# An embedding lookup with position add: the scheduled loop against five hand-written instruction streams

## The chip, the cores and the metric

The kernel runs on one core of a Trainium2 chip. The metric is the device time of one execution in microseconds (us). A profile covers one execution; its *span* runs from the first to the last instruction that it records. Differences of 2% count as faster or slower, smaller ones as the same.

Runs were made on several chips. The jobs fall into two kinds, told apart by SyncE's records at the end of the kernel: in one kind (called *slow SyncE* below, which is not the slow state of a run) they stand 0.70 us apart, in the other they take 7 to 28 ns. Times are therefore compared only within one job, where the kernel before was run beside the others; where two jobs are set side by side, the text says so.

## The reference

```python
batch, seq_len, vocab_size, d_model = 32, 512, 50000, 512
def reference(indices, embedding_table, position_embed):
    token_embed = embedding_table[indices]            # 32 x 512 rows of 512 floats
    return (token_embed + position_embed).astype(np.float32)
```

Rows of 2 KB are gathered (33.5 MB), the position rows added, and the result stored (33.5 MB).

## The kernel before

It is written for a scheduler (a tile framework) that puts in all waits. GpSimd gathers 128 rows for each instruction, VectorE adds, SyncE stores. A data tile holds up to four gathers; 20 tiles rotate. The waits are on *semaphores*, counters that one engine or DMA raises and another waits for.

```python
const = ctx.enter_context(tc.tile_pool(name="const", bufs=1))
data_pool = ctx.enter_context(tc.tile_pool(name="data", bufs=BUFS))   # BUFS = 20
# ... cut: load indices, transpose them, copy the position rows to PSUM (pos_ps)
def chunk(b, parts):
    at = 0
    for n in parts:
        data = data_pool.tile([P, n, D], f32, tag="data")
        for j in range(n):
            k = at + j
            where = idx0[:, 2 * k : 2 * k + 1] if b == 0 else idx_t[:, k, b : b + 1]
            nc.gpsimd.indirect_dma_start(out=data[:, j, :], out_offset=None, in_=table,
                in_offset=bass.IndirectOffsetOnAxis(ap=where, axis=0))
            nc.vector.tensor_tensor(out=data[:, j, :], in0=data[:, j, :],
                                    in1=pos_ps[k][:], op=add)
        nc.sync.dma_start(out=out_rows[b][:, at : at + n, :], in_=data[:])
        at += n
# batches 0, 1, 31: parts (1,1,1,1); 2 to 5 and 30: (2,2); all others: (4,)
```

## Time and profile before

| | |
|---|---|
| time, median of 3 runs | 184.62 us (184.57 to 184.68) |
| span of the profiled execution | 176.2 us |
| time of that same execution | 177.94 us |

The last two rows belong to one execution, the first to others.

These lines are from the profile page of the kernel before: the span, three rows of the span in 40 slices (busy tenths, and GB/s), the DMA packets, the chain of waits by engine, and the two costliest groups of instructions.

```profile
span 176.2 us, 480 instructions
...
POOL 3777777777777777777777777777777756777300
DMA  4889999999999999999999999999999999999995
GB/s 131 305 236 354 384 380 387 414 410 406 417 378 397 413 413 407 402 404 390 419 419 415 415 421 412 415 413 414 419 420 416 415 408 421 406 399 406 413 411 205
DMA packets 17635, 68.33 MB, mean 388 GB/s; under 512 B 3008, under 2 KB 3008, under 8 KB 14560
...
DMA 57%; POOL 27%; issue 11%; DVE 2%; POOLq 0%; DVEq 0%
...
L88 POOL DMA_INDIRECT data<-in_embedding_table_dram,idx_t x124 | 117.2, 945 | 39.8 <-issue 33.7
L94 DVE TENSOR_TENSOR data<-data,pos_ps 128x512 f32<-128x512 f32 x128 | 86.9, 687 | 79.6 <-DMA data<-in_embedding_table_dram,idx_t 72.7
```

DMA is at 9 tenths from the third slice to the next-to-last one. GpSimd (POOL) is at 7 tenths, and its idle time is mostly "issue": it waits for nothing that the profile shows.

This is the table of stages of the kernel before. The last two numbers of a line are the mean busy share of the DMA engines and GB/s.

```profile
0.00:5.00 5.00, 0.56 (x4) 0.55 (x4) 0.52 (x1) 1.73 (x2) 2.28 (x8) 1.00 0.48 141
10.00:15.00 5.00, 0.00 (x0) 0.00 (x0) 2.14 (x4) 0.00 (x0) 3.78 (x5) 1.00 0.93 275
40.00:60.00 20.00, 0.00 (x0) 0.00 (x0) 11.17 (x17) 0.00 (x0) 15.13 (x17) 1.00 1.02 402
140.00:160.00 20.00, 0.00 (x0) 0.00 (x0) 10.84 (x16) 0.00 (x0) 13.70 (x15) 1.00 1.02 410
170.00:174.00 4.00, 0.00 (x0) 0.00 (x0) 1.20 (x2) 0.00 (x0) 0.00 (x0) 1.00 1.01 397
174.00:175.00 1.00, 0.00 (x0) 0.00 (x0) 0.00 (x0) 0.00 (x0) 0.00 (x0) 1.00 0.19 72
175.00:176.20 1.20, 0.00 (x0) 0.00 (x0) 0.00 (x0) 0.00 (x0) 0.00 (x0) 1.00 0.00 0
```

The transfers run at full rate until 174 us and are over before 175 us. What follows is the *end*: 1.2 us without any transfer, in which the engines close down together.

The timeline of GpSimd in the kernel before, near its only stall (start, duration, instruction, idle time before it):

```profile
143.31 0.94 POOL L88 DMA_INDIRECT data<-in_embedding_table_dram,idx_t  x1 [0.35 <-issue]
146.37 0.95 POOL L88 DMA_INDIRECT data<-in_embedding_table_dram,idx_t  x1 [2.12 <-issue]
147.63 0.95 POOL L88 DMA_INDIRECT data<-in_embedding_table_dram,idx_t  x1 [0.30 <-DMA out_dram<-data]
```

And two lines of the kernel's closing instructions (source line 132, where the framework closes): duration in ns, minimum, median and maximum, then first and last start.

```profile
L132 SPq EVENT_SEMAPHORE  x12: 17/28/28, 172.3 to 176.2; - x12
L132 POOLq DRAIN  x3: 40/102/10675, 161.4 to 176.0; - x3
```

SyncE (SPq) goes through its twelve closing waits at 17 to 28 ns each.

### The profile page before, as it was taken

What the parts mean: (1) busy time and instruction counts of PE and PEld (TensorE: products, weight loads), DVE (VectorE), ACT (ScalarE), POOL (GpSimd) and SP (SyncE); (2) the same over time, 40 slices, a digit from 0 to 9 for tenths busy, and PEclk for the clock granted to TensorE, in tenths of its full rate; (3) what the DMA queues carried; (4) which work ended last, traced back from release to release, by engine and by line L of the source; (5) the groups of instructions that cost most, each with busy time, mean ns of one, the idle gap of its engine ahead of it and who ended that gap; (6) DMA issues with size and microseconds to landing.
All of it is one profiled execution on the core that took longest, in us unless ns stands there. A gap on an engine that the chain in (4) does not pass through costs nothing.

```text
span 176.2 us, 480 instructions
## 1 busy us (share of the span) xinstructions
PE 0.7 (0%) x4; PEld 0.6 (0%) x4; DVE 87.7 (50%) x130; ACT 3.6 (2%) x5; POOL 121.7 (69%) x134
## 2 busy tenths in 40 slices
PE   0100000000000000000000000000000000000000
PEld 0100000000000000000000000000000000000000
DVE  1162554454744447354466464544647464444740
ACT  2410000000000000000000000000000000000000
POOL 3777777777777777777777777777777756777300
DMA  4889999999999999999999999999999999999995
GB/s 131 305 236 354 384 380 387 414 410 406 417 378 397 413 413 407 402 404 390 419 419 415 415 421 412 415 413 414 419 420 416 415 408 421 406 399 406 413 411 205
DMA packets 17635, 68.33 MB, mean 388 GB/s; under 512 B 3008, under 2 KB 3008, under 8 KB 14560
## 3 DMA queue, kind: packets, MB, share of 16 engines
q0 software_dynamic: 10240, 33.56, 50.2%
q1 hardware_dynamic: 7392, 34.74, 48.1%
q14 instruction: 3, 0.02, 0.0%
HBM read 34.74 MB, written 33.55 MB: 388 GB/s over the span
## 4 chain that ended last, share of the span: by engine, by line
DMA 57%; POOL 27%; issue 11%; DVE 2%; POOLq 0%; DVEq 0%
DMA data<-in_embedding_table_dram,idx_t 56%; POOL data L88 27%; DVE data L94 2%; DMA idx<-in_indices_dram 1%; POOLq L88 0%; DVEq L94 0%
## 5 line engine op out<-in xcount | busy, mean ns | idle before, releaser
L88 POOL DMA_INDIRECT data<-in_embedding_table_dram,idx_t x124 | 117.2, 945 | 39.8 <-issue 33.7
L94 DVE TENSOR_TENSOR data<-data,pos_ps 128x512 f32<-128x512 f32 x128 | 86.9, 687 | 79.6 <-DMA data<-in_embedding_table_dram,idx_t 72.7
L88 POOL DMA_INDIRECT data<-in_embedding_table_dram,idx x4 | 4.0, 993 | 2.7 <-DMA idx<-in_indices_dram 1.7
L79 ACT COPY pos_ps<-pos_sb 128x512 f32<-128x512 f32 x4 | 2.4, 589 | 4.9 <-DMA pos_sb<-in_position_embed_dram 4.8
L68 DVE CAST idx_f<-idx_raw 32x512 f32<-32x512 int32 x1 | 0.5, 523 | 3.8 <-DMA idx_raw<-in_indices_dram 3.8
L79 ACT ACT_TABLE_LOAD x1 | 1.3, 1283 | 0.8 <-PEq L121 0.8
L75 DVE CAST idx_t<-turned 128x128 int32<-128x128 f32 x1 | 0.3, 292 | 0.8 <-PE turned L73 0.8
L73 PE MATMUL turned<-ident,idx_f 32*128 32x32 f32 x4 | 0.7, 300 | 4.4 <-DVE idx_f L68 4.4
L73 PEld LDWEIGHTS turned<-ident,idx_f 32*128 32x128 f32 x4 | 0.6, 206 | 4.4 <-issue 4.4
L121 POOL MEMSET const-float32-0.0<- 128x1 f32 x1 | 0.1, 105 | 0.3 <-issue 0.3
L60 POOL MEMSET ones<- 32x32 f32 x1 | 0.1, 114 | 0.3 <-POOLq L121 0.3
L62 POOL TENSOR_SCALAR_AFFINE_SELECT ident<-ones 32x32 f32<-32x32 f32 x1 | 0.2, 202 | 0.1
L121 POOL MEMSET const-uint8-127<- 128x1 uint8 x1 | 0.1, 122 | 0.0
L121 POOL MEMSET const-bfloat16-1.0<- 128x1 bf16 x1 | 0.1, 116 | 0.0
L121 POOL MEMSET const-float32-1.0<- 128x1 f32 x1 | 0.1, 108 | 0.0
## 6 DMA issues: line engine op xcount, KB each, us to landing
out_dram<-data SPq DMA_DIRECT2D x24, 1024.0 KB, 7.7
out_dram<-data SPq DMA_DIRECT2D x10, 512.0 KB, 6.9
out_dram<-data SPq DMA_DIRECT2D x12, 256.0 KB, 5.8
data<-in_embedding_table_dram,idx_t POOLq DMA_INDIRECT x124, 7.7
pos_sb<-in_position_embed_dram SPq DMA_DIRECT2D x4, 256.0 KB, 4.7
idx_raw<-in_indices_dram SPq DMA_DIRECT2D x1, 128.0 KB, 2.5
data<-in_embedding_table_dram,idx POOLq DMA_INDIRECT x4, 4.7
idx<-in_indices_dram SPq DMA_DIRECT2D x1, 4.0 KB, 1.8
```

Of the source, the lines that this page charges most:

```text
L60: nc.gpsimd.memset(ones[:], 1.0)
L62: nc.gpsimd.affine_select(out=ident[:], in_=ones[:], pattern=[[-1, B]], compare_op=mybir.AluOpType.is_equal, fill=0.0, base=0, channel_mul ...
L68: nc.vector.tensor_copy(out=idx_f[:].rearrange("b p k -> b (p k)"), in_=idx_raw[:, :, 0])
L73: nc.tensor.transpose(turned[:, k, :], idx_f[:, :, k], ident[:])
L75: nc.vector.tensor_copy(out=idx_t[:], in_=turned[:])
L79: nc.scalar.copy(out=pos_ps[k][:], in_=pos_sb[k][:])
L88: nc.gpsimd.indirect_dma_start(out=data[:, j, :], out_offset=None, in_=table, in_offset=bass.IndirectOffsetOnAxis(ap=where, axis=0),)
L94: nc.vector.tensor_tensor(out=data[:, j, :], in0=data[:, j, :], in1=pos_ps[k][:], op=add)
L121: nc = _bacc.Bacc("TRN2", target_bir_lowering=False, num_devices=1)
```

## The change

The intent is to take waiting and scheduling into the author's hands: one critical section, five instruction streams, a semaphore for each purpose, at most one wait on an instruction. There are 24 full slots instead of 20 tiles and 16 completion lanes for gathers instead of the framework's 8 (a *slot* is a buffer for one batch of four gathers; a *lane* is a semaphore that says that a gather has landed, and gathers take the lanes in turn). Stores are issued from ScalarE. Gathers, adds, store sizes and bytes stay.

```diff
-BUFS = 20
+SLOTS = 24
+LANES = 16
 ...
+    with tc.tile_critical():
+        nc.sync.dma_start(out=idx0[:], in_=idx_first).then_inc(s_first, 16)
 ...
+        for g in range(B * K):                                   # GpSimd
+            b, k = divmod(g, K)
+            if b >= SLOTS and k == 0:
+                nc.gpsimd.wait_ge(s_out[b - SLOTS], 16 * done)
+            ins = nc.gpsimd.indirect_dma_start(out=slots[b % SLOTS][:, k, :], ...
+            ).then_inc(s_gather[g % LANES], 16)
+            if g >= LANES:
+                ins._wait_ge(s_gather[g % LANES], rounds(g - LANES))
 ...
+            nc.vector.tensor_tensor(out=part, in0=part, in1=pos_ps[k][:], op=add
+            )._wait_ge(s_gather[g % LANES], rounds(g)).then_inc(s_add, 1)
 ...
-            nc.sync.dma_start(out=out_rows[b][:, at : at + n, :], in_=data[:])
+            nc.scalar.dma_start(out=out_rows[b][:, at : at + n, :],
+                in_=slots[b % SLOTS][:, at : at + n, :],
+            )._wait_ge(s_add, b * K + at + n).then_inc(done, 16)
+        nc.sync.wait_ge(s_rest, 16 * rest)
```

The last line: SyncE waits for the last stores.

More of the change, by code (lines that the diff above doesn't have):

```diff
@@ L9 @@
 K = 4
-BUFS = 20
+SLOTS = 24
+LANES = 16
+HALVES = (2, 2)
+QUARTERS = (1, 1, 1, 1)
 @with_exitstack
@@ L38 @@
     table = embedding_table[:, :]
-    const = ctx.enter_context(tc.tile_pool(name="const", bufs=1))
-    data_pool = ctx.enter_context(tc.tile_pool(name="data", bufs=BUFS))
-    psum = ctx.enter_context(
-        tc.tile_pool(name="psum", bufs=1, space=bass.MemoryType.PSUM)
-    )
-    idx0 = const.tile([P, 2 * K], i32)
-    nc.sync.dma_start(out=idx0[:], in_=idx_first)
-    idx_raw = const.tile([B, S, 2], i32)
-    nc.sync.dma_start(
-        out=idx_raw[:], in_=idx_words.rearrange("b (s w) -> b s w", w=2)
-    )
@@ L54 @@
-    pos_sb = [const.tile([P, D], f32, name=f"pos_sb{k}") for k in range(K)]
-    for k in range(K):
-        nc.sync.dma_start(out=pos_sb[k][:], in_=pos_rows[:, k, :])
-    ones = const.tile([B, B], f32)
-    nc.gpsimd.memset(ones[:], 1.0)
-    ident = const.tile([B, B], f32)
-    nc.gpsimd.affine_select(
-        out=ident[:], in_=ones[:], pattern=[[-1, B]],
-        compare_op=mybir.AluOpType.is_equal, fill=0.0, base=0,
-        channel_multiplier=1,
-    )
-    idx_f = const.tile([B, P, K], f32)
@@ L68 @@
-    nc.vector.tensor_copy(
-        out=idx_f[:].rearrange("b p k -> b (p k)"), in_=idx_raw[:, :, 0]
-    )
-    turned = psum.tile([P, K, B], f32)
-    for k in range(K):
-        nc.tensor.transpose(turned[:, k, :], idx_f[:, :, k], ident[:])
-    idx_t = const.tile([P, K, B], i32)
-    nc.vector.tensor_copy(out=idx_t[:], in_=turned[:])
-    pos_ps = [psum.tile([P, D], f32, name=f"pos_ps{k}") for k in range(K)]
-    for k in range(K):
-        nc.scalar.copy(out=pos_ps[k][:], in_=pos_sb[k][:])
@@ L81, in chunk, with sbuf, psum @@
-    def chunk(b, parts):
+    def sbuf(name, shape, dtype):
+        return ctx.enter_context(tc.tile_pool(name="p_" + name, bufs=1)).tile(
+            shape, dtype, name=name
+        )
+    def psum(name, shape, dtype):
+        pool = tc.tile_pool(name="p_" + name, bufs=1, space=bass.MemoryType.PSUM)
+        return ctx.enter_context(pool).tile(shape, dtype, name=name)
+    idx0 = sbuf("idx0", [P, 2 * K], i32)
+    idx_raw = sbuf("idx_raw", [B, S, 2], i32)
+    ones = sbuf("ones", [B, B], f32)
@@ new lines @@
+    ident = sbuf("ident", [B, B], f32)
+    idx_f = sbuf("idx_f", [B, P, K], f32)
+    idx_t = sbuf("idx_t", [P, K, B], i32)
+    pos_sb = [sbuf(f"pos_sb{k}", [P, D], f32) for k in range(K)]
+    slots = [sbuf(f"slot{n}", [P, K, D], f32) for n in range(SLOTS)]
+    turned = psum("turned", [P, K, B], f32)
+    pos_ps = [psum(f"pos_ps{k}", [P, D], f32) for k in range(K)]
+    stores = []
+    for b in range(B):
+        if b <= 1 or b == B - 1:
+            parts = QUARTERS
+        elif b <= 5 or b == B - 2:
+            parts = HALVES
+        else:
+            parts = (K,)
@@ L82, in chunk @@
         at = 0
         for n in parts:
-            data = data_pool.tile([P, n, D], f32, tag="data")
-            for j in range(n):
-                k = at + j
-                where = idx0[:, 2 * k : 2 * k + 1] if b == 0 else idx_t[:, k, b : b + 1]
-                nc.gpsimd.indirect_dma_start(
-                    out=data[:, j, :],
-                    out_offset=None,
-                    in_=table,
-                    in_offset=bass.IndirectOffsetOnAxis(ap=where, axis=0),
-                )
-                nc.vector.tensor_tensor(
-                    out=data[:, j, :], in0=data[:, j, :], in1=pos_ps[k][:], op=add
-                )
@@ L97, in chunk @@
-            nc.sync.dma_start(out=out_rows[b][:, at : at + n, :], in_=data[:])
-            at += n
-    for b in range(B):
-        if b <= 1 or b == B - 1:
-            chunk(b, (1, 1, 1, 1))
-        elif b <= 5 or b == B - 2:
-            chunk(b, (2, 2))
-        else:
-            chunk(b, (K,))
+            stores.append((b, at, n))
+            at += n
+    sem = tc.alloc_semaphore
+    s_first, s_raw = sem("s_first"), sem("s_raw")
+    s_pos = [sem(f"s_pos{k}") for k in range(K)]
+    s_gather = [sem(f"s_gather{n}") for n in range(LANES)]
@@ new lines, with rounds @@
+    s_out = {b: sem(f"s_out{b}") for b in range(B - SLOTS)}
+    s_rest = sem("s_rest")
+    s_ident, s_cast, s_turn, s_idx, s_ps, s_add = (
+        sem(n) for n in ("s_ident", "s_cast", "s_turn", "s_idx", "s_ps", "s_add")
+    )
+    def rounds(g):
+        return 16 * (g // LANES + 1)
+    with tc.tile_critical():
+        nc.sync.dma_start(out=idx0[:], in_=idx_first).then_inc(s_first, 16)
+        nc.sync.dma_start(
+            out=idx_raw[:], in_=idx_words.rearrange("b (s w) -> b s w", w=2)
+        ).then_inc(s_raw, 16)
+        for k in range(K):
+            nc.sync.dma_start(out=pos_sb[k][:], in_=pos_rows[:, k, :]).then_inc(
+                s_pos[k], 16
+            )
+        nc.gpsimd.memset(ones[:], 1.0).then_inc(s_ident, 1)
+        nc.gpsimd.affine_select(
+            out=ident[:], in_=ones[:], pattern=[[-1, B]],
+            compare_op=mybir.AluOpType.is_equal, fill=0.0, base=0,
+            channel_multiplier=1,
+        )._wait_ge(s_ident, 1).then_inc(s_ident, 1)
+        nc.gpsimd.wait_ge(s_first, 16)
+        for g in range(B * K):
+            b, k = divmod(g, K)
+            if g == K:
+                nc.gpsimd.wait_ge(s_idx, 1)
+            if b >= SLOTS and k == 0:
+                done = sum(1 for x in stores if x[0] == b - SLOTS)
+                nc.gpsimd.wait_ge(s_out[b - SLOTS], 16 * done)
+            where = idx0[:, 2 * k : 2 * k + 1] if b == 0 else idx_t[:, k, b : b + 1]
+            ins = nc.gpsimd.indirect_dma_start(
+                out=slots[b % SLOTS][:, k, :],
+                out_offset=None,
+                in_=table,
+                in_offset=bass.IndirectOffsetOnAxis(ap=where, axis=0),
+            ).then_inc(s_gather[g % LANES], 16)
+            if g >= LANES:
+                ins._wait_ge(s_gather[g % LANES], rounds(g - LANES))
+        nc.tensor.wait_ge(s_ident, 2)
+        for k in range(K):
+            ins = nc.tensor.transpose(turned[:, k, :], idx_f[:, :, k], ident[:])
+            ins.then_inc(s_turn, 1)
+            if k == 0:
+                ins._wait_ge(s_cast, 1)
+        nc.vector.tensor_copy(
+            out=idx_f[:].rearrange("b p k -> b (p k)"), in_=idx_raw[:, :, 0]
+        )._wait_ge(s_raw, 16).then_inc(s_cast, 1)
+        nc.vector.tensor_copy(out=idx_t[:], in_=turned[:])._wait_ge(
+            s_turn, K
+        ).then_inc(s_idx, 1)
+        for g in range(B * K):
+            b, k = divmod(g, K)
+            if b == 0:
+                nc.vector.wait_ge(s_ps, k + 1)
+            part = slots[b % SLOTS][:, k, :]
+            nc.vector.tensor_tensor(
+                out=part, in0=part, in1=pos_ps[k][:], op=add
+            )._wait_ge(s_gather[g % LANES], rounds(g)).then_inc(s_add, 1)
+        for k in range(K):
+            nc.scalar.copy(out=pos_ps[k][:], in_=pos_sb[k][:])._wait_ge(
+                s_pos[k], 16
+            ).then_inc(s_ps, 1)
+        rest = 0
+        for b, at, n in stores:
+            done = s_out.get(b, s_rest)
+            rest += done is s_rest
+            nc.scalar.dma_start(
+                out=out_rows[b][:, at : at + n, :],
+                in_=slots[b % SLOTS][:, at : at + n, :],
+            )._wait_ge(s_add, b * K + at + n).then_inc(done, 16)
+        nc.sync.wait_ge(s_rest, 16 * rest)
```

## The prediction

> **What bounds the kernel now.** The DMA engines. In the table of stages their busy share is 1.02 from 15 us to 165 us, at 402 to 415 GB/s from 30 us on; the page says 68.33 MB in all. At 412 GB/s that is 166 us of a 176.2 us span. The rest is the start (141 GB/s in the first 5 us, about 290 in the next 10) and the tail: the last add starts at 171.2 us, the rate is about 404 GB/s up to 173 us, then 359 and 72, and the last 1.2 us move nothing.
>
> A second clock ticks almost as fast: GpSimd issues a gather each 1.25 us (0.945 us busy, 0.30 us "issue"); 128 of them take 160 us. Each brings 256 KB in and causes 256 KB to go out, so 1.25 us asks for 419 GB/s, a hair above what the DMA delivers. Hence the chain of waits alternates between gathers' DMA time (56%) and GpSimd (27%). The 1.25 us is there in the first ten gathers, with little traffic, so it is the instruction's own cost. VectorE (50%) and ScalarE (2%) have room.
>
> The kernel has 8 completion lanes for gathers, so gather g waits for g-8, i.e. 10 us; landing takes 7.7 us median. In the timeline this bites only late: the issue distance is 1.33, 1.31, 1.30 us at 123, 133 and 143 us, then 3.06 us at 146 us. Together about 2.1 us; the DMA was busy throughout (1.02 share, 410 GB/s).
>
> **What the change does.**
> - Removes second and third waits of gathers and stores. A separate wait takes SyncE 17 ns, and three-wait gathers already keep the 1.25 us. Worth nothing.
> - 16 lanes and 24 slots for 20: removes the 2.1 us of GpSimd stalls. As the DMA has no gap there, this is not 2 us: raising 140-160 us from 410 to 415 GB/s gives 0.25 us, a fuller tail perhaps 0.3 us.
> - Stores from ScalarE. Its last position copy ends at 9.3 us, the first store was issued at 9.26 us: no delay. The Trainium skill, page "DMA: Bandwidth & Descriptors", section "Issuing engines are not separate DMA queues", says that all issuers end on the same 16 DMA engines and only sequencer time is saved. SyncE's 46 issues of 332 ns make 15 us of 176: nothing to save. I expect the same bandwidth.
> - The critical section adds a semaphore hop before SyncE's first load (0.1 to 0.3 us), and one before the closing barriers (0.2 to 0.5 us); estimates from the hops that the trace shows.
> - Bytes, gather shape, add and store sizes stay.
>
> **On the critical path:** minus about 0.5 us, plus about 0.4 us. Predicted 184.4 us, 80% range 183.0 to 185.8. Faster by over 2%: 0.06; within 2%: 0.90; slower: 0.04.
>
> **What would show it.** Right: gathers 0.945 us busy at distance 1.25 us, no 3 us gap near 146 us, DMA share 1.02 at 405 to 418 GB/s from 30 to 165 us; median landing of a gather 7.7 to 9 us; first gather at 3.0 to 3.3 us; span 175.5 to 176.8 us. Stores in their own queue, same bytes. Wrong: another gather distance, or a steady rate outside that band.
>
> **What would make it wrong.** Stores on their own queue that share the DMA engines differently with gathers (2% in rate is 3.3 us); gathers running ahead that starve stores, with waits for slots or a longer store tail; a costly entry or exit of the critical section (over 1 us); a faster start, where some 6 us are lost against the full rate.

## More of the kernel before

A *drain* (DRAIN in the profile) is an instruction in the list that closes each engine's stream.

GpSimd's long drain begins at 161.4 us, while transfers still run, so it costs nothing.

## The result

| | before | after |
|---|---|---|
| median | 184.59 us (4 runs) | 184.36 us (4 runs) |
| ratio after : before | | 0.9989, 95% interval 0.9972 to 1.0006 |
| spans of the timed runs | not kept | 182.4 to 182.6 us |

A ratio here is the mean time of one kernel's fast runs over that of the other's fast runs of the same rounds, so it is not quite the ratio of the medians. The class is "same", and the forecast of 184.4 us was met within 0.04 us.

The profile page of the changed kernel, the lines that answer those above:

```profile
span 182.6 us, 398 instructions
...
POOL 3777777777777777777777777777777777760000
DMA  4989999999999999999999999999999999999910
GB/s 127 303 236 373 363 396 389 414 384 408 406 387 406 376 407 416 418 420 413 415 417 413 417 404 425 410 415 418 413 423 401 424 405 417 415 415 417 397 64 0
...
POOL 64%; issue 23%; DMA 6%; DVE 1%; SPq 0%; POOLq 0%
...
L121 POOL DMA_INDIRECT slot<-in_embedding_table_dram,idx_t x124 | 117.5, 948 | 37.8 <-issue 37.8
L150 DVE TENSOR_TENSOR slot<-slot,pos_ps 128x512 f32<-128x512 f32 x128 | 87.1, 688 | 79.7 <-DMA slot<-in_embedding_table_dram,idx_t 47.2
```

The gather and the add cost what they did. Two things look new. The chain now says GpSimd 64%, and the span has grown by 6.4 us although the time has not. The first does not say by itself that GpSimd is the bound: the DMA share is 1.02 as before. Why the chain stays on GpSimd is open. This profile has no landing times for gathers and stores, but that is not the reason: after_copy, the same kernel profiled again, has them (8.5 us median for a gather, inside the 7.7 to 9 us forecast) and its chain says GpSimd 65%. The half_gather experiment below tests the question. The second is in the table of stages:

```profile
0.00:5.00 5.00, 0.33 (x3) 0.33 (x3) 0.42 (x1) 1.45 (x2) 2.14 (x8) 1.00 0.49 140
10.00:15.00 5.00, 0.00 (x0) 0.00 (x0) 2.18 (x4) 0.00 (x0) 3.78 (x5) 1.00 0.88 261
40.00:60.00 20.00, 0.00 (x0) 0.00 (x0) 11.76 (x18) 0.00 (x0) 15.12 (x17) 1.00 1.02 401
140.00:160.00 20.00, 0.00 (x0) 0.00 (x0) 10.51 (x17) 0.00 (x0) 15.12 (x17) 1.00 1.02 414
170.00:174.00 4.00, 0.00 (x0) 0.00 (x0) 1.38 (x2) 0.00 (x0) 0.00 (x0) 1.00 1.00 394
174.00:175.00 1.00, 0.00 (x0) 0.00 (x0) 0.00 (x0) 0.00 (x0) 0.00 (x0) 1.00 0.21 80
175.00:176.20 1.20, 0.00 (x0) 0.00 (x0) 0.00 (x0) 0.00 (x0) 0.00 (x0) 1.00 0.00 0
176.20:182.60 6.40, 0.00 (x0) 0.00 (x0) 0.00 (x0) 0.00 (x0) 0.00 (x0) 1.00 0.00 0
```

The transfers end before 175 us, as before. By the packet records the last store is done at 174.51 us (before: 174.69 us). All of the difference in span is the end, 8.1 us against 1.5 us.

GpSimd's timeline at the same place as before shows the stall gone:

```profile
143.57 0.94 POOL L121 DMA_INDIRECT slot<-in_embedding_table_dram,idx_t  x1 [0.30 <-issue]
144.82 0.96 POOL L121 DMA_INDIRECT slot<-in_embedding_table_dram,idx_t  x1 [0.30 <-issue]
146.08 0.94 POOL L121 DMA_INDIRECT slot<-in_embedding_table_dram,idx_t  x1 [0.30 <-issue]
```

Closing instructions of the changed kernel, at line 94 (the end of the critical section):

```profile
L94 SPq EVENT_SEMAPHORE  x3: 17/713/1397, 175.1 to 178.2; - x3
L94 POOLq DRAIN  x1: 2515/2515/2515, 175.2 to 175.2; - x1
```

Two costs are seen there. GpSimd's drain of 2.5 us starts at 175.2 us, after the last store. And SyncE's waits are now recorded at about 0.70 us, or twice that, instead of 28 ns.

### The profile page after: what moved, and what is told of

The parts are those of the page before. It is cut to its first block, busy times and chain, and to the rows that moved or that the text cites. A ratio compares the mean times of both kernels' runs of the same rounds, so it can differ in the third digit from the quotient of the medians.

```text
span 182.6 us, 398 instructions
## 1 busy us (share of the span) xinstructions
PE 0.7 (0%) x4; PEld 0.6 (0%) x4; DVE 87.8 (48%) x130; ACT 3.6 (2%) x5; POOL 122.1 (67%) x134
## 4 chain that ended last, share of the span: by engine, by line
POOL 64%; issue 23%; DMA 6%; DVE 1%; SPq 0%; POOLq 0%
POOL slot L121 64%; DMA slot<-in_embedding_table_dram,idx_t 5%; DVE slot L150 1%; DMA idx<-in_indices_dram 1%; SPq L193 0%; POOLq L119 0%; SPq L94 0%
## 5 line engine op out<-in xcount | busy, mean ns | idle before, releaser
L121 POOL DMA_INDIRECT slot<-in_embedding_table_dram,idx_t x124 | 117.5, 948 | 37.8 <-issue 37.8
L150 DVE TENSOR_TENSOR slot<-slot,pos_ps 128x512 f32<-128x512 f32 x128 | 87.1, 688 | 79.7 <-DMA slot<-in_embedding_table_dram,idx_t 47.2
L121 POOL DMA_INDIRECT slot<-in_embedding_table_dram,idx x4 | 4.0, 996 | 2.6 <-DMA idx<-in_indices_dram 1.7
```

Source lines behind the costliest of these rows:

```text
L121: ins = nc.gpsimd.indirect_dma_start(out=slots[b % SLOTS][:, k, :], out_offset=None, in_=table, in_offset=bass.IndirectOffsetOnAxis(ap=whe ...
L150: nc.vector.tensor_tensor(out=part, in0=part, in1=pos_ps[k][:], op=add)._wait_ge(s_gather[g % LANES], rounds(g)).then_inc(s_add, 1)
```

## The experiments

Theory: (a) up to the last store the kernel is bound by the DMA engines, so nothing that the change does there can be seen; (b) the change lets GpSimd's drain slip behind the last store; (c) in some jobs SyncE's last instructions are slow, in both kernels, and that hides (b). Rivals: the stores' new queue moved the rate; lanes and slots brought something that was lost elsewhere; the change is neutral everywhere.

### before_copy: the kernel before, again (chip 0)

No edit.

> The kernel before once more, unchanged, for its spans. Its only profile so far shows a span of 176.2 us with a time of 177.9 us, while its timed runs take 184.6 us; the changed kernel shows a span of 182.6 us with a time of 184.65 us. Theory A (the profile of the kernel before was an execution with an unusually short end): spans of the timed runs are near 182.8 us, some 1.8 us under their times, and a new profile shows a longer end after the last store. Theory B (its work really ends 6 us earlier, and the time holds something outside the span): spans stay near 176 us with times of 184.6 us.

Measured: 185.17 us, spans 183.3 to 183.6 us. Theory A of the expectation holds: a time is its span plus about 1.7 us, and the profile that I predicted from was an execution with a short end.

From the page and the closing instructions of this profile:

```profile
span 183.6 us, 480 instructions
...
L132 SPq EVENT_SEMAPHORE  x12: 1/694/699, 176.4 to 183.5; - x12
L132 POOLq DRAIN  x3: 40/102/11207, 161.1 to 183.3; - x3
L97 SPq DMA_DIRECT2D out_dram<-data x46: 332/332/1206, 10.3 to 175.0; - x46
```

The same twelve waits, 694 ns in the median instead of 28. The last store was done at 174.75 us, 0.05 us later than in the other profile of this kernel. So the kernel before spends 8.8 us at its end in this job and 1.5 us in the other profile.

What the 0.70 us are is not settled. The Trainium skill, page "Perfetto Trace Analysis", section "Summary: the profiler window per engine type", says that the recorded window of a sequencer-only instruction is its execution and leaves out its wait for a semaphore. These traces differ: in wait_act_b one SyncE wait for two semaphores is recorded with 2483 ns, from 172.84 us to 175.33 us, and ScalarE's drain that it waits for ends at 175.30 us. So a long record alone does not tell slow from waiting. Nor do the records tell when SyncE did its work: the last line above puts the start of the 46th store's issue at 175.0 us, but the last packet of all 46 stores ended at 174.75 us (in the kernel before's first profile that issue starts at 171.9 us). In that other profile the last packet ends 2.8 us after that start, so by an estimate the record is about 3 us late. The close is late as well: GpSimd, whose records are as short as ever, passes its last barrier wait at 183.4 us instead of 176.1 us. Whether SyncE is slow at its work, or held up by the recording of it, no run decides; all runs with a span on record were profiled.

### sp_stores: stores from SyncE (chip 0)

```diff
-            nc.scalar.dma_start(
+            nc.sync.dma_start(
```

> The changed kernel with its 46 stores issued from SyncE instead of ScalarE. Theory (all issuers share the same DMA engines, issue time is hidden): 184.4 us, within 0.3 us of the changed kernel, steady rate 402 to 417 GB/s. Rival (a queue of their own gives the stores another share of the engines, and something else took the gain back): a change of 1 us or more, in either direction, and another steady rate.

Measured: 184.69 us beside 185.19 us for the kernel before, ratio 0.9964 (0.9938 to 0.999). The changed kernel had 184.36 us and 0.9989 (0.9972 to 1.0006) beside the kernel before in its own job, where the kernel before was 0.6 us faster too. The last store is done at 174.81 us, and the rate from 80 to 160 us is 410 to 416 GB/s. The issuing engine is worth nothing measurable; the theory holds.

### half_gather: half the gathers, all stores (chip 0, wrong result on purpose)

```diff
-        for g in range(B * K):                  # gathers and adds
+        for g in range(B * K // 2):             # 64 instead of 128
-                in_=slots[b % SLOTS][:, at : at + n, :],
+                in_=slots[b // 2][:, at : at + n, :],   # each slot stored twice
 # ... cut: every second batch is gathered; GpSimd waits for no slot; all stores count on s_rest
```

> Wrong result on purpose: only every second batch is gathered and added, and each such batch is stored twice, so 64 gathers less (16.8 MB less to move) and the same 46 stores. Theory (bytes over the DMA rate set the time): minus 16.8 MB at 412 GB/s, that is 40.7 us less, about 144 us, rate still near 412 GB/s. Rival (the 1.25 us clock of GpSimd sets it, as the chain of waits after the change says with 64% GpSimd): minus 64 times 1.25 us, 80 us less, about 104 us.

Measured: 139.16 us, one run; the last store is done at 130.17 us, 44.3 us earlier than with all gathers. The bytes predicted 40.7 us less, GpSimd's clock 80 us less. Two lines of its table of stages show where the other 3.6 us come from: the rate is about 424 GB/s instead of about 412.

```profile
40.00:60.00 20.00, 0.00 (x0) 0.00 (x0) 7.12 (x11) 0.00 (x0) 15.12 (x17) 1.00 1.02 425
80.00:100.00 20.00, 0.00 (x0) 0.00 (x0) 6.88 (x10) 0.00 (x0) 5.68 (x6) 1.00 1.02 423
```

68.33 MB at 412 GB/s and 51.54 MB at 424 GB/s differ by 44.3 us. The second rate is this run's own, so this is a check of the sum and not a forecast. The share of the DMA engines is 1.02 in both kernels. So DMA time is the bound, whatever the chain says. The packet records show two parts of the higher rate. From 80 to 160 us of the changed kernel a gather's packet of 4096 bytes takes 164 ns on average (25.0 bytes per ns), a store's packet of 8192 bytes 312 ns (26.2 bytes per ns), so a larger share of stores raises the rate. And in half_gather, from 40 to 120 us, both kinds are faster, 159 and 310 ns. An estimate from these four times gives 0.8% for the mix alone and 2.3% for both; the rates of these stretches, 415 and 424 GB/s, differ by 2.2%. Why a gather's packet is faster there was not tested.

### wait_act: ScalarE waits for the last stores (chip 0)

```diff
-        nc.sync.wait_ge(s_rest, 16 * rest)
+        nc.scalar.wait_ge(s_rest, 16 * rest)
```

> The changed kernel, but ScalarE, which issued the stores, waits for their end instead of SyncE. Theory A (the end of 7.6 us is a matter of the closing barriers, whoever waits): 184.4 us, same 7 us between the last store and the end of the span. Theory C (the end is slow because SyncE had been idle for 170 us before its last instructions): still SyncE that has to pass the barriers, so at most 1 us less. If the end falls to 1 to 2 us, the waiting engine was the cause, and the time falls to about 178 us.

Measured: 182.86 us, ratio 0.987 (0.9853 to 0.9887) to the kernel before. The last store was done at 174.85 us, no earlier than elsewhere, so all of the gain is the end: 5.7 us instead of 8.1. None of the expected outcomes fits; they had left GpSimd out. Its first line here explains the gain:

```profile
L94 POOLq DRAIN  x1: 22103/22103/22103, 150.7 to 150.7; - x1
L193 POOLq EVENT_SEMAPHORE  x4: 17/17/17, 175.6 to 176.4; - x4
L193 SPq EVENT_SEMAPHORE  x2: 700/1056/1412, 176.4 to 179.9; - x2
```

SyncE no longer waits, so it lets the others into the closing sequence early. GpSimd's drain begins at 150.7 us and is over at 172.8 us, before the last store. The other two lines are the last barrier waits: GpSimd and all other engines but SyncE have closed by 176.5 us, as early as in a job with fast SyncE (176.4 us in wait_act_b); only SyncE's records go on, to 180.6 us.

### wait_pool: GpSimd made to wait as well (chip 11)

```diff
         nc.scalar.wait_ge(s_rest, 16 * rest)
+        nc.gpsimd.wait_ge(s_rest, 16 * rest)
```

> The variant in which ScalarE waits for the last stores (182.9 us), with GpSimd made to wait for them as well. In the changed kernel GpSimd's closing drain started only after the last store and took 2.5 us; in the ScalarE variant it started early and was over before. Theory (that drain is what the 1.8 us came from): back to 184.4 us, give or take 0.4, with a drain of about 2.5 us after 175 us. Rival (it was the number of SyncE instructions left, or the engine that waits): stays near 182.9 us.

Measured: 180.84 us, beside 177.95 us for the kernel before in the same job, ratio 1.0146 (1.0103 to 1.0189). This job is of the other kind: the kernel before has spans of 175.8 to 177.2 us in its timed runs. The absolute times of the expectation are therefore moot, but the drain is behind the last store again (174.84 us), and the kernel is 2.9 us slower than the one before, and 2.5 us slower than the variant without GpSimd's wait (178.32 us, run on the same chip in the next job). The rival, which was about slow SyncE instructions, was tested only where there are none.

```profile
L94 POOLq DRAIN  x1: 2515/2515/2515, 175.5 to 175.5; - x1
```

### ticks: 128 small waits on SyncE (chip 11)

```diff
+        for n in range(1, B * K + 1):
+            nc.sync.wait_ge(s_add, n)
         nc.scalar.wait_ge(s_rest, 16 * rest)
```

> The variant in which ScalarE waits for the last stores, with 128 small waits on SyncE, one for each add, as a probe of SyncE's speed over the whole run: a wait that takes 17 ns normally, 0.70 us where SyncE is slow. Theory T1 (SyncE is slow in a stretch of time that begins at about 168 to 176 us and ends at about 182.6 us, whatever runs): the probes show 17 to 30 ns up to about 168 us and 0.70 us after it, and the time is 183 to 184.5 us, as some more slow instructions stand before the end. Theory T2 (SyncE gets slow because it had little to do, so fetching its next instructions is slow): with work all along no slow instruction at all, and about 178.5 us.

Measured: 178.8 us beside 177.95 us, ratio 1.0057 (1.0002 to 1.0113), and no slow SyncE instruction. As no kernel showed one on this chip, this does not separate the two theories of SyncE's slowness: inconclusive. Of the 0.8 us, 0.6 us are in the end (2.1 us, against 1.5 us in the kernel before's first profile), and they fit the drain: SyncE now reaches the closing sequence only after the last add, so the drain starts at 173.0 us and ends at 175.5 us, somewhat after the last store (174.67 us).

### lanes8_slots12: fewer lanes and slots (chip 11)

```diff
-SLOTS = 24
-LANES = 16
+SLOTS = 12
+LANES = 8
```

> The changed kernel with 8 gather lanes and 12 slots instead of 16 and 24. Theory (lanes and slots are off the path, the DMA engines have work either way): one or a few gathers on GpSimd wait 1 to 3 us near 145 us, the last store lands within 0.4 us of 174.6 us, and the time is 184.4 us within 0.5. Rival (the larger numbers bring what the critical section costs): slower by 1 us or more.

Measured: 179.91 us, ratio 1.0102 (1.0063 to 1.0141) to the kernel before in its job. The stall of GpSimd comes back, small, at the same place, and moves nothing: the last store is done at 174.92 us, while the changed kernel, run again on the same chip in the next job, had 175.42 us (in the slowest of its six runs). The stall was weaker than expected, 0.78 us of idle time instead of 1 to 3 us.

```profile
145.18 0.95 POOL L121 DMA_INDIRECT slot<-in_embedding_table_dram,idx_t  x1 [0.78 <-issue]
```

Sixteen lanes and 24 slots are off the path up to the last store. With 8 lanes and 12 slots GpSimd's closing drain took 1.86 us instead of 2.52 us.

### long_ticks: a longer kernel (chip 11)

```diff
+        # ... cut: the 128 waits of ticks, the semaphores s_again, b = B - SLOTS + n, ScalarE's waits
+        for n in range(SLOTS):      # after all stores are done, store batches 8 to 31 again
+            nc.scalar.dma_start(out=out_rows[b][:, :, :], in_=slots[b % SLOTS][:, :, :]
+            ).then_inc(s_again[n], 16)
+        for n in range(SLOTS):
+            nc.sync.wait_ge(s_again[n], 16)
```

> The probe kernel, made longer: after all stores are done, the last 24 batches are stored once more from the slots (25.2 MB, right result), one SyncE wait for each of these stores. At 26.3 bytes per ns and engine, 421 GB/s, that is 60 us more, about 243 us. Theory T1 (slow in a fixed stretch of time): SyncE slow between about 168 and 183 us, and fast at the end, so that the end after the last store takes 1 to 4 us. Rival T3 (slow whenever the kernel comes to its end, whatever the time): SyncE fast until about 235 us, and 0.70 us per instruction at the end.

Measured: 243.28 us (243 was expected from bytes per ns alone), result right. SyncE was fast throughout, in a job where it is fast anyway: no answer to T1 against T3. The drain behind the last store again takes 2515 ns.

### after_copy and wait_act_b: both kernels in a job with fast SyncE (chip 11)

No edits: the changed kernel, and the variant in which ScalarE waits.

> The changed kernel once more, unchanged. The kernel before took 184.6 to 185.2 us where SyncE's last instructions took 0.70 us each, and 177.95 us on the chip of the last four runs, where they took 17 to 28 ns. If this job meets a chip of the second kind: theory (GpSimd's closing drain of 2.5 us now stands after the last store, the entry costs 0.2 us) about 180.6 us against 178.0 us, 1 to 2% slower, the rival (the change is neutral everywhere) 178.0 us. If it meets a chip of the first kind: 184.4 us against 184.9 us, as before.

> ScalarE waits for the last stores, once more, for what it is worth on this job's chip. Theory: on a chip with fast SyncE the drain is off the path again, so 178.0 us within 0.5 us of the kernel before; on a chip with slow SyncE 182.9 us, 1.3% under the kernel before. Rival (the gain of that run belonged to its chip's slow SyncE alone): slower than the kernel before by 1% or more on a fast chip.

Measured, six runs each, beside 178.13 us for the kernel before (11 runs): the changed kernel takes 180.72 us, ratio 1.0138 (1.0109 to 1.0166); the variant 178.32 us, ratio 1.0015 (0.9986 to 1.0044). Both expectations are met, and the rival "neutral everywhere" falls. Closing lines of the changed kernel in this job:

```profile
L94 SPq EVENT_SEMAPHORE  x3: 17/28/28, 176.0 to 176.2; - x3
L94 POOLq DRAIN  x1: 2515/2515/2515, 176.0 to 176.0; - x1
```

and of the variant:

```profile
L94 POOLq DRAIN  x1: 23332/23332/23332, 149.9 to 149.9; - x1
```

With SyncE at 28 ns, the drain of 2.5 us stands alone between the last store and the closing barriers, and the change is 1.4% slower.

### early_first: a shorter start (chip 12)

```diff
-            if b == 0:
-                nc.vector.wait_ge(s_ps, k + 1)
+            if b == 0:
+                nc.vector.wait_ge(s_pos[k], 16)     # read the position rows from SBUF
+            if b == 1:
+                nc.vector.wait_ge(s_ps, k + 1)
-            nc.scalar.dma_start(
+            (nc.sync if b == 0 else nc.scalar).dma_start(
 # ... cut: the first batch's adds take pos_sb[k] as their second input
```

> The variant in which ScalarE waits for the last stores, and the start shortened: the four adds of the first batch read the position rows from SBUF instead of waiting for ScalarE's copies, and its four stores go out from SyncE, so the first store can leave at about 8.6 us instead of 9.3 us. Theory (the start is short of work for the DMA engines, 0.82 to 0.94 busy between 8 and 13 us): at most 0.5 us less than the variant without it, so 177.8 us on a chip where the kernel before takes 178.1 us, 182.4 us on one where it takes 185 us. Rival (the start is limited by slow packets, not by missing work): no change, 178.3 us or 182.9 us.

Measured: 178.48 us beside 178.12 us, ratio 1.0026 (1.0003 to 1.0049): nothing gained. The test was also weaker than meant. The first store left at 9.15 us instead of the 9.29 us of the changed kernel's profile, because the first add started at 8.43 us: it was waiting for its gather, not for ScalarE's copy. What limits the start stays open.

### pool_pad: one more instruction on GpSimd for each gather (chip 12)

```diff
+            nc.gpsimd.memset(pad[:, g : g + 1], 0.0)
```

> The variant in which ScalarE waits for the last stores, with one memset of one element for each partition on GpSimd after each gather, about 0.1 us busy. Theory (GpSimd's 1.25 us per gather lies only 1% under the 1.263 us that the DMA engines need for 512 KB at 415 GB/s): a distance of 1.35 us or more between gathers, GpSimd becomes the bound, the last gather goes out at about 176 us or later, and the time grows by 10 us or more. Rival (the memset hides in the 0.30 us between two gathers): distance 1.25 us, time unchanged.

Measured: 178.84 us, one run, beside 178.12 us. The rival holds. Its timeline:

```profile
59.59 0.95 POOL L122 DMA_INDIRECT slot<-in_embedding_table_dram,idx_t  x1 [0.19 <-issue]
60.52 0.12 POOL L128 MEMSET pad<- 128x1 f32 x1
60.84 0.95 POOL L122 DMA_INDIRECT slot<-in_embedding_table_dram,idx_t  x1 [0.19 <-issue]
```

The memset takes 0.12 us, the gap falls from 0.30 to 0.19 us, and the distance stays 1.25 us. So this did not slow GpSimd's clock, and how close that clock is to being the bound was not measured.

### The ends side by side

"Last store" is the end of its last packet; the end is the span of the same profiled execution minus that, taken from unrounded figures.

| SyncE | kernel | last store | span | end |
|---|---|---|---|---|
| slow | before_copy | 174.75 | 183.6 | 8.8 |
| slow | changed kernel | 174.51 | 182.6 | 8.1 |
| slow | sp_stores | 174.81 | 182.8 | 8.0 |
| slow | wait_act | 174.85 | 180.6 | 5.7 |
| fast | before (first profile) | 174.69 | 176.2 | 1.5 |
| fast | after_copy | 175.42 | 179.6 | 4.2 |
| fast | wait_pool | 174.84 | 179.1 | 4.2 |
| fast | lanes8_slots12 | 174.92 | 178.5 | 3.6 |
| fast | half_gather (chip 0) | 130.17 | 137.1 | 6.9 |
| fast | wait_act_b | 174.69 | 176.4 | 1.7 |

Without half_gather, the last store moves by 0.9 us at most, and the end by 7.3 us. Where SyncE is fast, the end follows the length of GpSimd's drain: end less drain is 1.65 to 1.70 us in the four profiles in which the drain came after the last store (drains of 2.52, 2.52, 1.86 and 5.29 us, in the order of the table; 2.0 us in long_ticks, which closes after other waits), and the end is 1.5 to 1.7 us in the two in which it did not. No edit aimed at the drain's length alone, but this is what a drain that stands alone at the end would give.

## Why the prediction was right or wrong

The time was right: 184.4 us forecast, 184.36 us measured. Point by point:

- **The DMA engines are the bound.** Right. Share 1.02 in both kernels, and half_gather follows bytes over rate (44.3 us less; 40.7 forecast at the old rate) and not GpSimd's clock (80 us).
- **A rate of 405 to 418 GB/s from 30 to 165 us.** Nearly: 401 to 417. The stage from 40 to 60 us had 401 and is outside the band that the prediction set itself; in the kernel before that stage had 402.
- **GpSimd's 1.25 us is the instruction's own cost.** Right that it stays under the change: the distance is 1.25 us and the busy time 948 ns. That it was "a hair" from being the bound was not tested, as the memset hid in the gap.
- **The stall of 2.1 us goes and is worth about 0.25 us.** The stall went. With 0.78 us of idle time at that place (lanes8_slots12) the last store was no later. A gain of 0.25 us could not be told anyway from the 0.9 us by which the last store varies between the profiles of all variants (174.51 to 175.42 us).
- **Stores from ScalarE change nothing.** Right, by sp_stores: the ratio to the kernel before of the same job is 0.9964 with stores from SyncE and 0.9989 with stores from ScalarE, and the intervals overlap. The skill's statement that I cited agrees.
- **Entry of the critical section, 0.1 to 0.3 us.** Right: SyncE's first load starts at 1.02 us instead of 0.81 us, and the first gather at 3.08 us, within the 3.0 to 3.3 us forecast.
- **One hop before the closing barriers, 0.2 to 0.5 us.** Wrong; this is the step that failed. I counted the hop and overlooked what it holds back. In the kernel before, GpSimd's drain starts at 161.4 us under the last transfers. In the changed one SyncE lets the others into the closing sequence only after its own wait for the stores, so 2.5 us of drain come after the last store. wait_act takes it away, wait_pool brings it back, after_copy and wait_act_b show it without slow SyncE instructions: 180.72 against 178.32 us.
- **Extra waits are "worth nothing" as SyncE does one in 17 ns.** Not so with slow SyncE. There the kernel before's closing list is recorded at 0.70 us each, and it ends 8.8 us after the last store. The changed kernel has a shorter list and ends 8.1 us after it, although it also pays for the drain. That this shorter list is what offset the drain fits both tables; no run changed the length of the list alone in such a job, so it is argued and not shown.
- **Span 175.5 to 176.8 us.** Wrong: 182.6 us. I had taken the span of one execution and the time of others as one set of numbers. The execution's own time, 177.94 us, was beside it: time minus span is 1.7 us there, so a time of 184.6 us had to hold over 6 us that the profile before did not show.

In sum, the forecast was right about everything up to the last store, which is 95% of the time. At the end it missed a loss of 2.5 us, and that the number came out so closely is luck. With slow SyncE the kernel before's end is 7.3 us longer (8.8 us less 1.5) and the changed one's 3.9 us (8.1 less 4.2): these 3.4 us cover the 2.7 us by which the changed kernel's end is longer where SyncE is fast. These differences are taken between jobs. In a job of the fast kind the change made the kernel 1.4% slower, where the forecast was about no change; that is clear of the noise, though still inside the 2%.

What stays open: why SyncE's records stand 0.70 us apart in some jobs, and whether the 7 us would be there without a profile. In before_copy they were slow from 168.0 us on; in the changed kernel still fast at 175.2 us and slow from 176.1 us; in half_gather, on the same chip 0, SyncE was fast at its end near 137 us. The probes meant to settle this ran in jobs without it.

The best version found is wait_act: 1.3% under the kernel before where SyncE is slow, and level with it (1.0015, 0.9986 to 1.0044) where it is fast.

## What to carry to other kernels

Here the transfers filled the DMA engines almost from end to end, and hand-placed waits, more lanes and another issuing engine moved nothing; in such a kernel, look at the first and the last microseconds instead. Put the final wait on an engine whose arrival does not hold back the others' closing drains, and check in the trace that GpSimd's drain starts before the last store lands. Compare the profiled execution's own time with the timed ones before reading a span: a difference of 6.7 us meant here that they were not the same kind of execution. And check a record against what it must precede: a store's issue that is recorded after the store's last packet shows that the records of that engine are late.

## What the Trainium skill lacked or had wrong

- "VectorE: DVE Perf Modes", section "The DRAIN you can't avoid": it calls the drains of preamble and postamble about 12 ns, constant, on all five engines. Most closing drains of ScalarE and SyncE agree (7 to 14 ns, where SyncE is fast). GpSimd's does not: 2515 ns in five of the profiles in which it came after the last store, 1862 ns with 8 gather lanes and 12 slots, and 5292 ns in half_gather. No run here shows what sets these values.
- "Perfetto Trace Analysis", section "Summary: the profiler window per engine type", leaves the wait for a semaphore out of a sequencer-only instruction's window. A SyncE wait for two semaphores was recorded with 2483 ns here, nearly all of it waiting (see before_copy).
- No page that I read tells that SyncE's closing instructions can be recorded at 0.70 us each in some jobs (12 waits of 694 ns in the median against 28 ns), with 7 us more of the same kernel's time, or that these records can come after the work that they stand for.
- No page that I read gives the pace of indirect gathers. A gather of 128 rows keeps GpSimd for 0.945 us and comes every 1.25 us, 160 us for 128 of them.
- "Perfetto Trace Analysis", section "Roofline", puts the ceiling of one core's 16 DMA engines at about 435 GB/s and does not tell how far a mix of gathers and stores stays below it; the highest sustained rate here is 425 GB/s, with stores at two thirds of the bytes, and 401 to 417 GB/s from 40 us on with half gathers and half stores (the changed kernel).
